# Branch B's product by seven half-size products per column pair, its weight sums in DRAM, and moved stores and bounds

## The chip, the cores and the metric

One core of a Trainium2 chip runs the kernel. The metric is the device time of one execution in microseconds (us). Each core has a matrix engine (TensorE, PE in the profile, with its weight loads as PEld), a vector engine (DVE), a scalar engine (ACT), GpSimd (POOL) and a queue engine (SP) that here only issues DMAs. Every engine works through its own instructions in order and waits on semaphores for the others.

## The reference

One layer of a trunk, on x of 512 × 2048 in float32. Two branches share an RMS-normalised input h: a gated DeltaNet (A) and a convolution module (B). What matters here:

```python
u = jax.nn.glu(glu_in, axis=-1)
u = causal_depthwise_conv(u, w_dw[i]) + b_dw[i]
u = jax.nn.silu(layernorm(u, ln_g[i], ln_b[i])) * jax.nn.silu(z_b)
y_b = u @ w_br_b[i]

gate_a, gate_b = jnp.split(jax.nn.sigmoid(gate_logits + b_gate[i]), N_BRANCHES, axis=-1)
mixed = (gate_a * y_a + gate_b * y_b) @ w_out[i]
x = x + rmsnorm(mixed, g_post[i])

e = p[i] @ w_ple_proj[i]
x = x + rmsnorm(jax.nn.sigmoid(x @ w_ple_gate[i]) * e, g_ple[i])
```

y_a, made by branch A, is `o_a @ w_br_a`. All weights of these products are 2048 × 2048.

## The kernel before

**Arithmetic.** Every product is made of three matmuls on split operands. A float32 operand becomes a high part (a cast on ACT, line 126 for a weight) and a low part (the rest, a subtraction on DVE, line 127); high × high, high × low and low × high are added up in PSUM. A weight piece of 128 × 512 goes SP load (`raw`, three buffers of two pieces) → ACT → DVE into a ring of four pieces `w`; `next_piece()` keeps three made ahead of the one in use.

**Stages.** The load of x, its norm, and p · w_ple_proj (up to 46 us; the product e is kept in SBUF and stored to `pe_dram` by sixteen DMAs on POOL's queue, line 309); the gate and z projections; the heads of branch A with the projections of q, k and v (565 to 1480); GLU and depthwise convolution (to about 1830); branch A's product; layer norm; branch B's product (1902 to 2085); the out product with w_out; the last stage with w_ple_gate.

**Seven products.** The gate and z projections and the out product are already made, per pair of column blocks, of seven half-size products instead of eight: with 512 rows as two halves and the columns as two, sums of operand blocks (S1 to S4) meet sums of weight blocks. For the out product the weight sums are formed beforehand in DRAM: `presum` (lines 1057 and 1062) copies and adds blocks of w_out with 64 DMAs on POOL's queue during the heads (48 read w_out, 16 copy a sum), one per 30 matmuls. The operand blocks come from the merged gate result `mixed` (called gt): `turned` transposes it through PE (tp, line 1275), `combine_low` and `combine_high` (lines 1288 to 1314) form A11, S1 to S4 and the casts (oph, line 1260; opl, line 1262). The product itself is f, lines 1430 to 1432, with weight pieces of 128 × 1024 (wsp, lines 1411 and 1412).

**Branch B before.** `branch()` is the plain product: four column blocks j in the order 0, 2, 1, 3; each of 16 steps takes one weight piece for four row tiles × three matmuls, twelve in all (yp, lines 1136, 1138, 1140). `evac_yb` multiplies by the gate (line 1246) and adds to `mixed` (line 1250). Its operands u come from the layer norm: a sum by a matmul with ones (sum_ps, 1189), mean and variance (1196 to 1204), a diagonal matrix dg (1211), the inverse deviation spread by a matmul (rstd_ps, 1216, at 1872.8), then for each of 16 channel tiles a product with it (1220), silu on ACT (1221), the product with zb (1225), the cast (1227) and the low part (1229).

**Order.** Work beside the matmuls is written as generators: `spawn(gen, period)` enters one, and every matmul calls `tick()`, which steps each generator once per so many matmuls. The Tile context then schedules each engine's instructions; `pin` (keep_in_program_order) holds one where the program has it. `split_mixed()`, the generator of the combine parts, is spawned after the first column block of branch B (period 10) and carried to its end in the out product's opening by `stepper`. There the order is: pair 0's P1 and P7, pair 1's P1, then the rest of pair 0, then Q5, P6, P3, P2, P7, Q4 of pair 1. `post(LOW)`, which norms the first rows and transposes them (line 1521), is stepped under pair 1's P7 and Q4.

Of the kernel before, what the change touches and what calls it, by code (L numbers as in the profile page):

```python
# [81 lines left out]
def _body(ctx, tc, A, out):  # L82
# [155 lines left out]
    def load_x():  # L238
        with tc.tile_pool(name="xin", bufs=1) as xin, tc.tile_pool(name="xps", bufs=6, space=PSUM) as xps:
# [68 lines left out]
            for (j, tt), e in e_sb.items():  # L308
                nc.gpsimd.dma_start(pe_dram[j, tt], e)
# [426 lines left out]
    def head_scan(g, hh, G):  # L736
# [56 lines left out]
        for tt in range(NTT):  # L793
            nc.tensor.transpose(po[:, tt].rearrange("p x i -> p (x i)"), O[:, tt, :], ident)
# [384 lines left out]
    def layer_norm():  # L1179
# [9 lines left out]
        mm(pm, ones, acc[0], start=True, stop=True)  # L1189
# [26 lines left out]
        mm(rstd, ones, dg, start=True, stop=True)  # L1216
# [27 lines left out]
    def evac_yb(j, tt, ps):
        gt = gate_b[tt][j]
        nc.vector.tensor_tensor(gt, ps, gt, ALU.mult)
        if tt == NTT - 1:
            for t in range(NTT):
                m = mixed[t][j]
                nc.vector.tensor_tensor(m, m, gate_b[t][j], ALU.add)  # L1250
            added[j] = NTT


# [74 lines left out]
    def load_gate_b(j):  # L1328
        for tt in range(NTT):
            gate_b[tt][j] = s2.tile([P, T], F32, tag="s2", name="gb")  # L1330
            nc.sync.dma_start(gate_b[tt][j], g_dram[1, tt, j])

    def wanted(k):
        while uT[min(k + 1, NK - 1)] is None:
            next(norm)

    mix = split_mixed()
    for n, j in enumerate((0, 2, 1, 3)):
        for q in range(4):
            if q == 1:  # L1340
                jobs.append(lambda j=j: load_gate_b(j))
            branch(A["w_br_b"], j, q, uT, evac_yb, wanted if n == 0 else None)
        if n == 0:
            jobs.append(lambda: finish())
            jobs.append(lambda: spawn(mix, 10, "mix"))
# [11 lines left out]
    LOW, HIGH, ALL = (0, 1), (2, 3), (0, 1, 2, 3)  # L1357
    SLOT, HP_, S3_ = (slots, "s"), (hpool, "h"), (s3, "s3")

    def unit(home, name, dt=F32):  # L1360
        return home[0].tile([P, T], dt, tag=home[1], name=name)
# [144 lines left out]
    def post(tts, xr):  # L1506
# [7 lines left out]
        for j in range(4):  # L1514
            if j < 3:
                with_x(j + 1)
            for k2 in (2 * j, 2 * j + 1):
                ps = bank()
                for n in range(4):
                    k = 2 * k2 + n // 2  # L1520
                    nc.tensor.transpose(ps[:, n * P:(n + 1) * P], x1[tts[n % 2]][j][:, (k % 4) * P:(k % 4 + 1) * P], ident)
# [232 lines left out]
```

## Time and profile before

| what | value |
|---|---|
| median of 3 runs | 2430.66 us (2429.46 to 2431.43) |
| the profiled execution | 2433.04 us, span 2431.3 |
| granted TensorE clock, mean | 0.998 |
| busy: PE, PEld, DVE, ACT, POOL | 99%, 82%, 75%, 48%, 19% |

The profile is that of one execution. Busy times are sums over instructions; matmuls overlap one another (one lasts 0.39 us, the next begins 0.23 us after it), so PE's pace is read from counts in a window of time, not from durations. A line such as `L1250 ... x3` in a timeline is three instructions in a row, with the time from the first's start to the last's end. In square brackets stands the idle time ahead of an instruction, and what ended it.

### The profile page before, as it was taken

How to read it: one execution, taken by the hardware profiler on the slowest of the kernel's cores; microseconds unless marked ns; L12 is line 12 of the kernel's file. 1: busy time of each engine (PE TensorE's matmuls, PEld its weight loads, DVE VectorE, ACT ScalarE, POOL GpSimd, SP SyncE). 2: the span in 40 equal slices, each digit the busy share in tenths (PEclk: the TensorE clock that was granted, in tenths of full speed). 3: DMA queues.
4: the chain of work that ended last, by engine and by line, in shares of the span. 5: the costliest groups of instructions: out<-in, count | busy, mean ns of one | idle time of the engine just before them, and what ended most of it. 6: DMA issues, size and time to landing. Idle time of an engine off the chain costs nothing.

```text
span 2431.3 us, 33577 instructions
## 1 busy us (share of the span) xinstructions
PE 2411.2 (99%) x11966; PEld 1985.0 (82%) x11966; DVE 1811.8 (75%) x3376; ACT 1163.3 (48%) x2331; POOL 449.8 (19%) x449
## 2 busy tenths in 40 slices
PE   9999999999999999999999999999999999999998
PEld 7888888887888888888888887888887888888886
DVE  7877888776778686777868678999998654667644
ACT  6555455555554545454554544454424433554532
POOL 2001100011112121121101001998840000000000
PEclk9999999999999999999999999999999999999999
DMA  6477766764364463554323221443434332664552
GB/s 264 158 193 212 200 199 202 208 171 161 130 174 143 139 192 127 151 161 136 116 76 102 76 84 69 156 139 104 163 128 164 128 129 100 230 226 164 193 175 77
DMA packets 133145, 371.80 MB, mean 153 GB/s; under 512 B 14833, under 2 KB 23281, under 8 KB 132465
## 3 DMA queue, kind: packets, MB, share of 16 engines
q1 hardware_dynamic: 116848, 315.12, 38.2%
q0 software_dynamic: 13824, 50.34, 9.4%
q10 hardware_dynamic: 2304, 4.20, 0.5%
q8 instruction: 94, 1.54, 0.2%
q14 instruction: 75, 0.61, 0.1%
HBM read 338.14 MB, written 65.01 MB: 166 GB/s over the span
## 4 chain that ended last, share of the span: by engine, by line
PE 92%; DVE 4%; DMA 2%; issue 1%; ACT 1%; POOL 0%; SPq 0%; DVEq 0%; POOLq 0%; ACTq 0%
PE g L185 14%; PE g L187 14%; PE g L183 14%; PE zp L475 6%; PE zp L473 6%; PE zp L474 6%; PE yp L1140 4%; PE yp L1138 4%; PE yp L1136 4%; PE f L1431 2%; PE f L1432 2%; PE f L1430 2%; PE f L1605 2%; PE f L1603 2%; PE f L1604 2%; PE psB L760 1%
## 5 line engine op out<-in xcount | busy, mean ns | idle before, releaser
L185 PE MATMUL g<-hl,w 128*128 128x512 f32 x1536 | 610.5, 397 | 0.0
L187 PE MATMUL g<-hh,w 128*128 128x512 f32 x1536 | 609.0, 397 | 0.0
L183 PE MATMUL g<-hh,w 128*128 128x512 f32 x1536 | 608.3, 396 | 0.0
L126 ACT CAST w<-raw 128x512 fp32r<-128x512 f32 x580 | 356.2, 617 | 525.6 <-PE g L187 258.5
L127 DVE TENSOR_TENSOR w<-raw,w 128x512 fp32r<-128x512 f32 x466 | 321.4, 694 | 194.7 <-ACT w L126 192.2
L185 PEld LDWEIGHTS g<-hl,w 128*128 128x128 f32 x1536 | 289.2, 188 | 55.4 <-issue 1.2
L183 PEld LDWEIGHTS g<-hh,w 128*128 128x128 f32 x1536 | 289.3, 188 | 53.9
L187 PEld LDWEIGHTS g<-hh,w 128*128 128x128 f32 x1536 | 289.3, 188 | 53.9 <-POOL w L127 0.3
L1006 DVE SCALAR_TENSOR_TENSOR uc<-up,vec,uc 128x497 f32<-128x497 f32 (+29 forms) x390 | 282.3, 734 | 13.2 <-ACT uc L985 1.9
L127 POOL TENSOR_TENSOR w<-raw,w 128x512 fp32r<-128x512 f32 x114 | 146.8, 1305 | 59.6 <-ACT w L126 57.8
L707 DVE SCALAR_TENSOR_TENSOR cv<-g,vec,cv 128x511 f32<-128x511 f32 x144 | 106.6, 740 | 41.4 <-ACT cv L705 41.1
L1138 PE MATMUL yp<-w,uh 128*128 128x512 f32 x256 | 100.4, 392 | 0.0
L1136 PE MATMUL yp<-w,uh 128*128 128x512 f32 x256 | 100.3, 393 | 0.1
L1140 PE MATMUL yp<-w,ul 128*128 128x512 f32 x256 | 100.4, 392 | 0.0
L1138 PE MATMUL yp<-w,oh 128*128 128x512 f32 x256 | 100.1, 391 | 0.0
L1140 PE MATMUL yp<-w,ol 128*128 128x512 f32 x256 | 99.5, 391 | 0.0
L1136 PE MATMUL yp<-w,oh 128*128 128x512 f32 x256 | 99.1, 389 | 0.0
L893 DVE TENSOR_TENSOR prod<-UT,VT 128x2 f32<-128x2 f32 (+30 forms) x248 | 87.3, 352 | 6.5
L718 POOL COPY kq<-kc 128x512 f32<-128x512 f32 x16 | 11.5, 721 | 383.9 <-ACT kc L716 225.5
L1028 POOL TENSOR_TENSOR uc<-uc,pr 128x511 f32<-128x511 f32 (+29 forms) x60 | 76.1, 1269 | 8.3 <-ACT pr L1027 7.7
L1430 PE MATMUL f<-wsp,oph 128*128 128x512 f32 x192 | 75.5, 393 | 0.0
L1603 PE MATMUL f<-w,xh 128*128 128x512 f32 x192 | 75.5, 393 | 0.0
(399 smaller groups left out, 4883.6 us busy)
## 6 DMA issues: line engine op xcount, KB each, us to landing
raw<-in_w_in SPq DMA_DIRECT2D x194, 512.0 KB, 3.3
wo_sums<-in_w_out POOLq DMA_DIRECT2D x48, 512.0 KB, 7.7
raw<-in_w_ple_gate SPq DMA_DIRECT2D x40, 512.0 KB, 3.3
raw<-in_w_br_a SPq DMA_DIRECT2D x32, 512.0 KB, 3.3
raw<-in_w_br_b SPq DMA_DIRECT2D x32, 512.0 KB, 3.3
raw<-in_w_ga SPq DMA_DIRECT2D x24, 512.0 KB, 5.1
raw<-in_w_gb SPq DMA_DIRECT2D x24, 512.0 KB, 5.1
raw<-in_w_z SPq DMA_DIRECT2D x22, 512.0 KB, 4.6
```

The costliest lines, as they stand in the source:

```text
L126: nc.scalar.copy(hi, rq)
L127: low_part[0].tensor_tensor(lo, rq, hi.bitcast(F32), ALU.subtract)
L183: mm(ps, wh, rh, start=(k == 0), stop=False)
L185: mm(ps, wh, rl, start=False, stop=False)
L187: mm(ps, wl, rh, start=False, stop=(k == NK - 1))
L473: mm(ps[pr][t], lh, wh, start=q + n == 0, stop=False)
L474: mm(ps[pr][t], ll, wh, start=False, stop=False)
L475: mm(ps[pr][t], lh, wl, start=False, stop=q == 3 and n == 1)
L1006: pin(nc.vector.scalar_tensor_tensor(y[:, s:], u[:, 0:T - s], vv(w0 + TAPS - 1 - s), y[:, s:], ALU.mult, ALU.add))
L1136: mm(ps[tt], lh[:, b], wh, start=k == 0, stop=False)
L1138: mm(ps[tt], lh[:, b], wl, start=False, stop=False)
L1140: mm(ps[tt], ll[:, b], wh, start=False, stop=k == NK - 1)
```

## The change

It makes these edits:

1. The sixteen stores of e leave `load_x` for a generator `stores()` in the next phase, each pinned.
2. Pins on the first matmuls of sw_ps, sum_ps, rstd_ps, on one transpose of po and on the transposes of `post`; one `yield` becomes `yield 14`.
3. Branch B's product is made of seven half-size products for each of the two column pairs. P1, P2 and Q4 run both pairs interleaved; Q5, P6, P7 and P3 follow for pair 0, then for pair 1. A weight piece serves two row tiles, six matmuls. The layer norm gives, for the first eight channel tiles, split halves (ua), and behind its loop the operands S1 to S4 (half-size sums `usf` on DVE, each pair of halves then cast and split, oph and opl). Results of a product are kept (`bsnap`, copied by ACT), combined, gated and added to `mixed` on DVE.
4. w_br_b is laid out in blocks, and its sums are formed in DRAM by the same `presum`, ahead of those of w_out: 64 more DMAs on POOL's queue, one per 24 matmuls.
5. `split_mixed` does all four `combine_low` and then all four `combine_high`; it is spawned after pair 0's P3 (period 7).
6. In the out product pair 1's P7 moves up, behind its P1, and its result is kept (s7b); `stepper` takes two steps in the first P1.

The core of the diff:

```diff
-            for (j, tt), e in e_sb.items():
-                nc.gpsimd.dma_start(pe_dram[j, tt], e)
...
+        def stores():
+            for (j, tt), e in e_sb.items():
+                pin(nc.gpsimd.dma_start(pe_dram[j, tt], e))
+                yield
+        spawn(stores(), 12, "form")
         spawn(gen, 7, "form")
...
-        mm(pm, ones, acc[0], start=True, stop=True)
+        pin(mm(pm, ones, acc[0], start=True, stop=True))
...
+    sums_b = dram.tile([2, 4, 4, P, 1024], F32, name="wb_sums")
+
+    def presums():
+        yield from presum(A["w_br_b"], sums_b)
+        yield from presum(WO, sums)
...
-            jobs.append(lambda: spawn(presum(WO, sums), 30, "presum"))
+            jobs.append(lambda: spawn(presums(), 24, "presum"))
...
-            uh = low(0, "uh")
-            nc.scalar.copy(uh, u)
-            ul = low(LOP if i < 33 - LOP else 0, "ul")
-            nc.vector.tensor_tensor(ul, u, uh.bitcast(F32), ALU.subtract)
+            if i < 8:
+                if i % 2 == 0:
+                    ua[i // 2] = low(0, "uh"), low(0, "ul")
+                c = slice((i % 2) * 256, (i % 2) * 256 + 256)
+                uh, ul = [x[:, c] for x in ua[i // 2]]
+                nc.scalar.copy(uh, u[:, LO])
+                nc.vector.tensor_tensor(ul, u[:, LO], uh.bitcast(F32), ALU.subtract)
+            else:
+                uh, ul = low(0, "uh"), low(LOP if i == NK - 1 else 0, "ul")
+                nc.scalar.copy(uh, u)
+                nc.vector.tensor_tensor(ul, u, uh.bitcast(F32), ALU.subtract)
             uT[i] = (uh, ul)
             yield 6
+        us1, us3 = [None] * 4, [None] * 4
+        for name in ("S1", "S2", "S3", "S4"):
+            for k2 in range(4):
...
+                for kk, c in halves(k2):
+                    u, v = u_t[kk], u_t[kk + 8]
+                    a, b, op = {"S1": (u[:, HI], v[:, HI], ALU.subtract), "S2": (t[:, c], u[:, LO], ALU.subtract),
+                                "S3": (u[:, LO], u[:, HI], ALU.subtract), "S4": (t[:, c], v[:, LO], ALU.add)}[name]
+                    nc.vector.tensor_tensor(t[:, c], a, b, op)
+                yield 4
+                uS[name][k2] = sw_split(*((s2, "s2") if name == "S1" else (hpool, "h") if name == "S3" else (lop, "lop")), t)
+                yield 6
...
+    def fin_b(tts, j, cs):
+        for tt, c in zip(tts, cs):
+            nc.vector.tensor_tensor(c, c, gate_b[tt][j], ALU.mult)
+        for tt, c in zip(tts, cs):
+            m = mixed[tt][j]
+            nc.vector.tensor_tensor(m, m, c, ALU.add)
+            added[j] += 1
...
     def split_mixed():
-        for part, k2 in ((combine_low, 0), (combine_low, 1), (combine_high, 0), (combine_high, 1),
-                         (combine_low, 2), (combine_low, 3), (combine_high, 2), (combine_high, 3)):
-            yield from part(k2)
+        for part in (combine_low, combine_high):
+            for k2 in range(4):
+                yield from part(k2)
...
+            for q in range(4):
+                for x, (jp, pr) in enumerate(products):
+                    for n in range(2):
+                        kk = 2 * q + n
+                        wh, wl = next_piece()
+                        for t in range(2):
+                            lh, ll = b_opnd(OPND[pr], kk, t)
+                            mm(ps[x][t], lh, wh, start=kk == 0, stop=False)
+                            tick()
+                            mm(ps[x][t], ll, wh, start=False, stop=False)
+                            tick()
+                            mm(ps[x][t], lh, wl, start=False, stop=kk == 7)
+                            tick()
...
+        def p7(jp):
+            def f(ps):
+                u = b_u[jp]
+                u3 = [tt_b(u["u2"][t], ps[t], u["u2"][t], ALU.add) for t in range(2)]
+                fin_b(HIGH, 2 * jp + 1, [tt_b(u["s5"][t], u["s5"][t], u3[t], ALU.subtract) for t in range(2)])
+                fin_b(HIGH, 2 * jp, [tt_b(u["s4"][t], u["s4"][t], u3[t], ALU.add) for t in range(2)])
+            return f
...
+        b_job([(0, "P1"), (1, "P1")], p1, [(S2_, LOW, 0), (S2_, LOW, 2)])
+        b_job([(0, "P2"), (1, "P2")], p2)
+        b_job([(0, "Q4"), (1, "Q4")], q4)
+        jobs.append(lambda: finish("norm"))
+        for jp in range(2):
+            b_job([(jp, "Q5")], q5(jp))
+            b_job([(jp, "P6")], p6(jp), [(LO_, HIGH, 2 * jp + 1), (LO_, HIGH, 2 * jp)])
+            b_job([(jp, "P7")], p7(jp))
+            b_job([(jp, "P3")], p3(jp), [(LO_, LOW, 2 * jp + 1)])
+            if jp == 0:
+                jobs.append(lambda: spawn(mix, 7, "mix"))
...
-    for jp, prs in ((0, ("P1", "P7")), (1, ("P1",)), (0, ("P2", "Q5", "P6", "P3", "Q4")), (1, ("Q5", "P6", "P3", "P2", "P7", "Q4"))):
+    for jp, prs in ((0, ("P1", "P7")), (1, ("P1", "P7")), (0, ("P2", "Q5", "P6", "P3", "Q4")), (1, ("Q5", "P6", "P3", "P2", "Q4"))):
...
-    ps = run(("P1",), stepper(gen))
+    ps = run(("P1",), stepper(gen, 2))
...
     pgen = post(LOW, xr)
-    ps = run(("P7",), stepper(pgen))
-    u3 = [add(u2[t], ps["P7"][t], u2[t]) for t in range(2)]
+    u3 = [add(u2[t], s7b[t], u2[t]) for t in range(2)]
...
-        "w_br_b": _tm_tiles(a["w_br_b"]),
+        "w_br_b": _sw_tiles(a["w_br_b"]),
```

The scheduler's order at three places. First POOL at the start of the kernel, before (xrs are the powers of the norm of x, each after its tile's statistics; the DMA rows are the stores of e):

```order
L309 DMA pe_dram<-e_sb 128x512 x2
L265 ISA
L265 TENSOR_TENSOR xrs<-xms,mhalf_c 128x1 x2
L309 DMA pe_dram<-e_sb 128x512 x4
L265 TENSOR_TENSOR xrs<-xms,mhalf_c 128x1
L309 DMA pe_dram<-e_sb 128x512 x6
```

And POOL there with the change:

```order
L101 MEMSET mhalf_c 128x8
L265 ISA
L265 TENSOR_TENSOR xrs<-xms,mhalf_c 128x1 x4
L507 DMA pe_dram<-e_sb 128x512 x16
L419 DMA zt<-in_w_z 128x512 x16
L419 DMA zt<-in_w_ga 128x512 x16
```

The stores, which stood between the powers, now stand behind all four of them and ahead of the z weights' sums.

Second DVE at the end of the layer norm, before (ur and ul are the tiles of u and their low parts, w weight pieces, zb the silu of z_b):

```order
L1220 TENSOR_TENSOR ur_16804<-ur_16804,rstd_ps_17098 128x512
L127 TENSOR_TENSOR w_17584<-raw_17582,w_17584 128x512
L127 TENSOR_TENSOR w_17587<-raw_17582,w_17587 128x512
L1225 TENSOR_TENSOR ur_16804<-ur_16804,zb_17438 128x512
L127 TENSOR_TENSOR w_17624<-raw_17622,w_17624 128x512
L1229 TENSOR_TENSOR ul_17508<-ur_16804,uh_17506 128x512
L127 TENSOR_TENSOR w_17627<-raw_17622,w_17627 128x512
```

And DVE there with the change (usf are the sums S1 to S4, opl their low parts):

```order
L1231 TENSOR_TENSOR ur_16869<-ur_16869,rstd_ps_17163 128x512
L127 TENSOR_TENSOR w_17631<-raw_17629,w_17631 128x512
L127 TENSOR_TENSOR w_17634<-raw_17629,w_17634 128x512
L1236 TENSOR_TENSOR ur_16869<-ur_16869,zb_17495 128x512
L1262 TENSOR_TENSOR usf_17639<-ur_16498,ur_16524 128x256
L1262 TENSOR_TENSOR usf_17639<-ur_16501,ur_16676 128x256
L1262 TENSOR_TENSOR usf_17656<-ur_16505,ur_16855 128x256
L1247 TENSOR_TENSOR ul_17564<-ur_16869,uh_17563 128x512
L1262 TENSOR_TENSOR usf_17656<-ur_16508,ur_16869 128x256
L127 TENSOR_TENSOR w_17661<-raw_17659,w_17661 128x512
L1305 TENSOR_TENSOR opl_17590<-usf_17581,oph_17588 128x512
```

Behind the last channel tile DVE had only weight pieces to make; now the sums and low parts of the four operands stand between these pieces.

Third DVE at the end of branch B's product, before (gb the gates, gt the merged result, yp the banks of PSUM, wsp the out product's weight pieces):

```order
L1246 TENSOR_TENSOR gb_18612<-yp_18496,gb_18612 128x512
L1246 TENSOR_TENSOR gb_18614<-yp_18497,gb_18614 128x512
L1250 TENSOR_TENSOR gt_17260<-gt_17260,gb_18610 128x512
L1250 TENSOR_TENSOR gt_17262<-gt_17262,gb_18612 128x512
L1250 TENSOR_TENSOR gt_17264<-gt_17264,gb_18614 128x512
L1412 TENSOR_TENSOR wsp_18840<-raw_18825,wsp_18839 128x1024
L1412 TENSOR_TENSOR wsp_18846<-raw_18827,wsp_18845 128x1024
L1262 TENSOR_TENSOR opl_18867<-sf_17846,oph_18865 128x512
L1262 TENSOR_TENSOR opl_18976<-tp_18963,oph_18974 128x512
```

And DVE at the end of pair 1's P7 with the change (bsnap the kept and combined results):

```order
L1294 TENSOR_TENSOR gt_17321<-gt_17321,bsnap_18750 128x512
L1294 TENSOR_TENSOR gt_17323<-gt_17323,bsnap_18752 128x512
L1433 TENSOR_TENSOR bsnap_18235<-bsnap_18235,bsnap_17859 128x512
L1433 TENSOR_TENSOR bsnap_18237<-bsnap_18237,bsnap_17861 128x512
L1291 TENSOR_TENSOR bsnap_18235<-bsnap_18235,gb_18758 128x512
L1291 TENSOR_TENSOR bsnap_18237<-bsnap_18237,gb_18760 128x512
L1294 TENSOR_TENSOR gt_16927<-gt_16927,bsnap_18235 128x512
L1294 TENSOR_TENSOR gt_16929<-gt_16929,bsnap_18237 128x512
L127 TENSOR_TENSOR w_18990<-raw_18985,w_18990 128x512
L127 TENSOR_TENSOR w_19026<-raw_19024,w_19026 128x512
L1305 TENSOR_TENSOR opl_19013<-tp_18998,oph_19011 128x512
L1305 TENSOR_TENSOR opl_19017<-tp_19003,oph_19015 128x512
```

The gates and adds of two column blocks (bsnap with gb, then gt) stand here ahead of the last weight pieces (w) of branch B and of the first low parts that combine_high makes from the transposes (opl from tp). Before, the last gates stood beside the out product's first pieces.

More of the change, by code (lines that the diff above doesn't have):

```diff
@@ L663, in beta_decay @@
         nc.vector.tensor_scalar(neg_eg.rearrange("p t h -> p (t h)"), eg, -1.0, None, ALU.mult)
-        yield
+        yield 14
         pw = wps.tile([P, T], F32, tag="w", name="sw_ps")
-        mm(pw[:, 0:n], cc(C_SWAP), eg, start=True, stop=True)
+        pin(mm(pw[:, 0:n], cc(C_SWAP), eg, start=True, stop=True))
         nc.vector.tensor_copy(eg_sw.rearrange("p t h -> p (t h)"), pw[:, 0:n])
@@ L793, in head_scan @@
         for tt in range(NTT):
-            nc.tensor.transpose(po[:, tt].rearrange("p x i -> p (x i)"), O[:, tt, :], ident)
+            turn = nc.tensor.transpose(po[:, tt].rearrange("p x i -> p (x i)"), O[:, tt, :], ident)
+            if tt == 0 and g == NH // 2 - 1:
+                pin(turn)
         yield
@@ L1215, in layer_norm @@
         rstd = ups.tile([P, T], F32, tag="u", name="rstd_ps")
-        mm(rstd, ones, dg, start=True, stop=True)
+        pin(mm(rstd, ones, dg, start=True, stop=True))
         yield 6
@@ L1225, in layer_norm @@
             nc.vector.tensor_tensor(u, u, zb[i], ALU.mult)
[L1226 to L1229 removed]
+            if i < 8:
[9 more added lines that the diff above has]
+                nc.vector.tensor_tensor(ul, u, uh.bitcast(F32), ALU.subtract)
             uT[i] = (uh, ul)
             yield 6
+        us1, us3 = [None] * 4, [None] * 4
+        for name in ("S1", "S2", "S3", "S4"):
+            for k2 in range(4):
+                if name == "S1":
+                    us1[k2] = hp("usf")
+                elif name == "S3":
+                    us3[k2] = hp("usf")
+                t = us3[k2] if name == "S3" else us1[k2]
+                for kk, c in halves(k2):
[6 more added lines that the diff above has]
+                yield 6
     def load_zb(i):
@@ L1235, in load_zb @@
         nc.sync.dma_start(zb[i], zb_dram[i])
+    ua = [None] * 4
+    uS = {n: [None] * 4 for n in ("S1", "S2", "S3", "S4")}
     norm = layer_norm()
@@ L1242, in _body, with unit, gate_in @@
     added = [0] * 4
[L1244 to L1251, printed above, removed]
+    SLOT, HP_, S2_, LO_ = (slots, "s"), (hpool, "h"), (s2, "s2"), (lop, "lop")
+    def unit(home, name, dt=F32):
+        return home[0].tile([P, T], dt, tag=home[1], name=name)
+    def gate_in(home, tts, j):
+        for tt in tts:
+            gate_b[tt][j] = unit(home, "gb")
+            nc.sync.dma_start(gate_b[tt][j], g_dram[1, tt, j])
+    def fin_b(tts, j, cs):
[5 more added lines that the diff above has]
+            added[j] += 1
     AW = {n: [None] * 4 for n in ("A11", "S1", "S2", "S3", "S4")}
@@ L1326, in split_s3 @@
             yield
[L1328 to L1331, printed above, removed]
+    WB = A["w_br_b"]
+    WHICH_B = {"P1": (WB, B11), "P2": (WB, B21), "P3": (WB, B22),
+               "Q5": (sums_b, T1), "P6": (sums_b, T2), "P7": (sums_b, T3), "Q4": (sums_b, T4)}
     def wanted(k):
-        while uT[min(k + 1, NK - 1)] is None:
+        while uT[k] is None:
             next(norm)
-    mix = split_mixed()
@@ L1338, in _body, with b_opnd @@
-    for n, j in enumerate((0, 2, 1, 3)):
-        for q in range(4):
[L1340 to L1345, printed above, removed]
+    def b_opnd(name, kk, t):
+        if name in ("A12", "A22"):
+            wanted(kk + 8)
+            c = (256 if name == "A22" else 0) + t * P
+            return [x[:, c:c + P] for x in uT[kk + 8]]
+        c = (kk % 2) * 256 + t * P
+        if name == "A11":
+            wanted(kk)
+            return [x[:, c:c + P] for x in ua[kk // 2]]
+        while uS[name][kk // 2] is None:
+            next(norm)
+        return [x[:, c:c + P] for x in uS[name][kk // 2]]
@@ new lines, in _body, with b_bank, b_job, job @@
+    b_banks = [0]
+    def b_bank():
+        b_banks[0] += 1
+        return yps.tile([P, T], F32, tag="y", name="yp")
+    def b_job(products, done_, gates=()):
+        for q in range(4):
+            for jp, pr in products:
+                W, blk = WHICH_B[pr]
+                prep_src.append(W[jp, blk, q])
+        def job():
+            for g_ in gates:
+                gate_in(*g_)
+            ps = [[b_bank() for _ in range(2)] for _ in products]
+            for q in range(4):
[11 more added lines that the diff above has]
+                            tick()
+            done_(*ps)
+        jobs.append(job)
@@ L1346, in _body @@
+    mix = branch_b()
     lnp_ctx = ExitStack()
@@ L1356, in _body @@
     fsm = ctx.enter_context(tc.tile_pool(name="fsm", bufs=1))
[L1357 to L1361, printed above, removed]
+    ALL = (0, 1, 2, 3)
+    S3_ = (s3, "s3")
     def bcast_row(src, j, home=S3_):
@@ L1547, in _body @@
     ps = run(("P1",), stepper(gen, 2))
+    s1b = [snap(SLOT, x) for x in ps["P1"]]
+    ps = run(("P7",), stepper(gen, 2))
     drain(gen)
-    s1b = [snap(HP_, x) for x in ps["P1"]]
+    s7b = [snap(S3_, x) for x in ps["P7"]]
     ps = run(("P2",))
```

40 lines of the change are left out of this document (39 added, 1 removed).

## The prediction

> **What bounds the kernel now.** I read the page's head first, then the chain that ended last, then TensorE's rate stretch by stretch. The page gives the span, the busy shares, and the chain by engine:
>
> ```profile
> span 2431.3 us, 33577 instructions
> PE 2411.2 (99%) x11966; PEld 1985.0 (82%) x11966; DVE 1811.8 (75%) x3376; ACT 1163.3 (48%) x2331; POOL 449.8 (19%) x449
> PE 92%; DVE 4%; DMA 2%; issue 1%; ACT 1%; POOL 0%; SPq 0%; DVEq 0%; POOLq 0%; ACTq 0%
> ```
>
> TensorE (PE) is the bound almost throughout, so a matmul taken away is worth its pitch if nothing else then comes late. The windows give that pitch, and show how near the vector engine (DVE) is to being the bound around branch B's product (columns: window, length, then busy time and count of PE, PEld, DVE, ACT, POOL; granted clock; DMA share; GB/s):
>
> ```profile
> 300.00:400.00 100.00, 100.00 (x443) 82.81 (x442) 82.22 (x132) 52.61 (x88) 7.06 (x8) 1.00 0.65 195
> 1880.00:1900.00 20.00, 20.00 (x90) 16.57 (x89) 18.55 (x32) 14.20 (x23) 0.00 (x0) 1.00 0.57 196
> 1900.00:1920.00 20.00, 19.88 (x86) 15.46 (x85) 16.91 (x28) 10.79 (x17) 0.00 (x0) 1.00 0.47 161
> 1920.00:1940.00 20.00, 20.00 (x90) 16.57 (x89) 4.85 (x7) 4.96 (x8) 0.00 (x0) 1.00 0.28 93
> 2080.00:2100.00 20.00, 20.00 (x94) 16.54 (x93) 16.30 (x22) 11.16 (x16) 0.00 (x0) 1.00 0.68 261
> 2100.00:2120.00 20.00, 19.75 (x92) 16.20 (x91) 18.38 (x28) 14.97 (x22) 0.00 (x0) 1.00 0.77 279
> ```
>
> 443 matmuls in 100 us are 225.7 ns each. Branch B's product begins near 1902. Just ahead of it DVE is full (18.55 of 20: the layer norm's tail), in its middle nearly idle (4.85), and at its end, where the operands of the out product are formed, full again (18.38). So DVE's spare time lies in the middle, and the change adds DVE work at both ends. All waits of PE in before over 0.25 us that bear on the change:
>
> ```profile
> PE xp L313 <- DVE hl L317: 3.6, 1, 3.6
> PE rstd_ps L1216 <- DVE dg L1211: 0.7, 1, 0.7
> PE f L1521 <- DVE c L1511: 0.6, 1, 0.6
> PE tp L1275 <- DVE sf L1314: 0.3, 1, 0.3
> ```
>
> Only the first is worth naming; the seams around branch B are crossed today almost without a stall.
>
> **The matmuls: −21.7 us.** Branch B was 4 column blocks × 16 × 4 × 3 = 768 matmuls and becomes 7 products × 2 column pairs × 8 × 2 × 3 = 672. 96 × 225.7 ns = 21.7 us. The f products and the 64 turning transposes keep their counts.
>
> **The stores at the start: −4.8 us.** The stretch where PE waits 3.6 us (windows, the chain, the DMA issues, and four transposes of the chain at full clock):
>
> ```profile
> 20.00:30.00 10.00, 10.00 (x51) 8.38 (x50) 8.99 (x19) 8.39 (x14) 6.28 (x10) 1.00 1.03 414
> 38.00:40.00 2.00, 2.00 (x9) 1.47 (x8) 2.00 (x4) 2.00 (x5) 0.00 (x0) 0.70 0.63 188
> 40.00:42.00 2.00, 2.00 (x9) 1.70 (x8) 2.00 (x4) 0.42 (x1) 0.00 (x0) 0.50 0.27 111
> 20.59 14.56 DMA raw<-in_w_in
> 43.31 0.44 PE xp L313 x4
> pe_dram<-e_sb POOLq DMA_DIRECT2D x16, 256.0 KB, 7.8
> 27.24 0.57 POOL L265 TENSOR_TENSOR xrs<-xms,mhalf_c 128x1 f32<-128x1 f32 x1 [0.59 <-DVE xms L263]
> L421 POOL DMA_DIRECT2D zt<-in_w_z x16: 865/890/1180, 115.8 to 216.8; - x16
> ```
>
> The DMA engines are full (1.03, 414 GB/s), and a weight load takes 14.56 us. The sixteen stores are 4.2 MB, 10 us of that bandwidth, ahead of or beside the last loads. With the change they stand behind the fourth power on POOL, which runs at 27.24 now and a little sooner then, so the loads land before PE asks. What goes is the 3.6 us and the half clock that follows it: 2 × 0.30 + 2 × 0.50 = 1.6 us. That is 5.2 at best; POOL issues eight of the stores without a wait, 2 MB or 5 us of bandwidth that may still meet the last load, so the low end is 1. I take 4.8, near the upper end, since the loads then have 10 us in hand against those 5. The stores' reader comes only in the last stage, and POOL's next work behind them, the z weights' sums, runs from 115.8 us on (the last row).
>
> The Trainium skill ("TensorE: Matmul & The Clock Gate", Part 1) puts the half clock down to an idle window of about 3.4 us; the trace agrees, with 0.50 after the one wait of 3.6. By it the clock is lost at any new wait of that length; that is a rival below.
>
> **The pins** (the waits for sw_ps, po, sum_ps, rstd_ps and the post transposes): in the order of the program these matmuls stand where they stood, so 0, and ±0.3 by the waits listed.
>
> **The norm's tail and the first two products: +7.8 us.** This needs DVE's pace when it runs without a break (first rows: consecutive starts; then the tail):
>
> ```profile
> 2100.04 2.36 DVE L1412 TENSOR_TENSOR wsp<-raw,wsp 128x1024 fp32r<-128x1024 f32 x2
> 2102.32 0.68 DVE L1262 TENSOR_TENSOR opl<-sf,oph 128x512 fp32r<-128x512 f32 x1
> 2102.92 1.22 DVE L1412 TENSOR_TENSOR wsp<-rw,wsp 128x1024 fp32r<-128x1024 f32 x1
> ...
> 2111.04 0.74 DVE L1306 TENSOR_TENSOR sf<-cm,tp 128x256 f32<-128x256 f32 x2
> 2111.70 1.22 DVE L1412 TENSOR_TENSOR wsp<-raw,wsp 128x1024 fp32r<-128x1024 f32 x1
> ...
> 1872.70 0.69 DVE L127 TENSOR_TENSOR w<-raw,w 128x512 fp32r<-128x512 f32 x1
> 1874.00 1.88 DVE L1220 TENSOR_TENSOR ur<-ur,rstd_ps 128x512 f32<-128x512 f32 x3 [0.62 <-PE rstd_ps L1216]
> 1882.73 1.40 DVE L1225 TENSOR_TENSOR ur<-ur,zb 128x512 f32<-128x512 f32 x2 [1.44 <-ACT ur L1221]
> 1902.11 0.68 DVE L1147 TENSOR_TENSOR gt<-yp,gt 128x512 f32<-128x512 f32 x1
> 1902.71 1.28 DVE L1225 TENSOR_TENSOR ur<-ur,zb 128x512 f32<-128x512 f32 x2
> 1903.91 0.68 DVE L1147 TENSOR_TENSOR gt<-yp,gt 128x512 f32<-128x512 f32 x1
> 1915.61 0.69 DVE L127 TENSOR_TENSOR w<-raw,w 128x512 fp32r<-128x512 f32 x1
> ```
>
> One 128x512 takes 0.68 alone and starts 0.60 before the next (2102.32 to 2102.92); two 128x1024 start 2.28 before what follows, 1.14 each; two 128x256 take 0.66, 0.33 each. In before DVE works from 1872.70 to 1916 and then rests. In the order of the change, from that same weight piece (at 1872.70) to the piece that P2's fifth step needs stand 125 DVE instructions: 85 of 128x512 (29 weight pieces, 32 norm products, 8 full low parts, 12 low parts of the sums, 4 gates of branch A) and 40 of 128x256 (8 half low parts, 32 of the sums S1 to S4). 85 × 0.60 + 40 × 0.33 = 64.2, with the two waits quoted (0.62, 1.44) 66.3: done at 1939.0. PE stands 250 matmuls behind the rstd matmul (about 1873.9) there: 1930.3 at full pace. It waits 8.7, of which before has about 0.9 (x86 against x90 in 1900 to 1920): +7.8. Bounds 5 and 12: two breaks like the 1.44 fewer or three more.
>
> **End of pair 0's P7: +2.9 us.** Behind P7's last matmul stand 16 DVE instructions of 128x512 (differences, gates, adds, the piece between): 16 × 0.60 + 0.7 of handing over = 10.3 before the transposes of the merged columns and the next piece are served; PE comes there after some 33 matmuls, 7.4. The pieces made ahead (3 × 6 × 0.2257 = 4.1) lie inside those 7.4. Bounds 0 and 5.
>
> **End of pair 1's P7, into the out product: +10.0 us.** With combine_high for all four column pairs now behind branch B, DVE has 38 × 0.60 + 12 × 0.33 + 6 × 1.14 = 33.6 us from P7's end to the last S4 sum that the 97th matmul after it waits for; PE's 97 matmuls and 16 transposes (0.11 each, from the four in 0.44) take 21.9 + 1.8 = 23.7. Before crossed this at 0.3. Bounds 6, if a tenth of the block is done while P7 still runs, and 14, at full single durations.
>
> **The rest.** The last stage's post(LOW) loses P7 as cover: +0.5 over the 0.6 quoted. The 64 sums of w_br_b go over POOL's queue in the heads stage: there PE is as dense with such copies as without (0.52 and 0.25 of the DMA engines):
>
> ```profile
> 900.00:1100.00 200.00, 200.00 (x1205) 165.73 (x1204) 147.38 (x363) 100.73 (x266) 32.47 (x40) 1.00 0.52 156
> 1200.00:1400.00 200.00, 200.00 (x1203) 165.79 (x1203) 147.72 (x351) 103.16 (x268) 15.77 (x19) 1.00 0.25 85
> L126 ACT CAST w<-raw 128x512 fp32r<-128x512 f32 x122 | 75.3, 620 | 135.3 <-PE yp L1140 106.7 <-PE f L1605 12.6 <-DVE w L127 8.2
> raw<-in_w_br_b SPq DMA_DIRECT2D x28, 512.0 KB, 3.2
> ```
>
> So 0. The raw loads double in rate (a piece now serves 6 matmuls, 1.35 us, and a load two pieces, 2.7 us) with three buffers: 8.1 us a round against 3.2 to land and two casts and two subtractions, 2.5. Covered; if it weren't, this is a ring that runs late in the whole product. For handshakes I don't see, +0.5. ACT's snapshots replace DVE reads of PSUM and lie under its idle time (it waits 106.7 us for PE there).
>
> **Sum.** −21.7 − 4.8 + 7.8 + 2.9 + 10.0 + 0.5 + 0.5 = −4.8. The profiled run took 2433.04, giving 2428.2; it lies 2.4 over the median of the three runs, 2430.66, so on the median's footing 2425.9, said as 2426. A change of under 0.2% (4.9 us) can't be told from none: faster means under 2425.8, slower over 2435.5. The forecast falls on that edge, and that is why its chances split.
>
> **The rivals.**
>
> *DVE can't hold the 0.60 pitch (chance 0.11).* The pitch holds between instructions that wait for nothing; the new ones wait for ACT's cast of the same tile each time. If each costs its single duration (0.68, 0.41, 1.22), the seams grow by 125 instructions' worth, 85 × 0.08 + 40 × 0.08 = 10.0, then 16 × 0.08 = 1.3, then 4.5: 15.8 in all, 2442, slower than before. It decides once two thirds of that comes. Against it: from 1902.11 to 1903.91 three instructions of two lines, on tiles that PE and ACT had written, took 1.80; for it: the 1.44 quoted. The Trainium skill ("VectorE: DVE Perf Modes", on SBUF-source latency) gives (N+151)/0.96 ns for such an add, 691 at 512; the trace agrees for a single one (0.68 to 0.69 us), not for a row of them.
>
> *The seams cost half (0.14).* If PE finds more made ahead than I counted, 20.7 of seams are 10 and the time is 2415; none at all would be 2404. For it: before crossed similar blocks of eight instructions with no wait. Against it: DVE's queue is in order and the counts are fixed.
>
> *The stores still collide (0.11).* Eight go out unhindered; if they meet the last weight load, the start keeps its 3.6 and its clock: 2431. It is also the case in which that edit doesn't do what it says.
>
> *The clock drops at the new waits (0.12).* The first and third seams may hold a wait of over 3.5 us; each then costs 2 us as at 38 to 42 (x9 for x18): 2430. Against it: PE would be slow where DVE is the bound anyway.
>
> **Chances and range.** The forecast has 0.52, spread over 2420 to 2432, half of it on each side of the edge. Faster: 0.26 + 0.14 + 0.02 + 0.03 (parts of the last two) = 0.45; same: 0.26 + 0.09 + 0.09 = 0.44; slower: 0.11. The range takes in the forecast, the two 2430 cases, half of the second rival, and the edge of the first: 2415 to 2437.
>
> **What would show it.** In the profile of the change: no wait at xp, granted clock 1.00 in 36 to 44, the stores issued after 24 us; 96 fewer PE instructions and the same 225.7 ns in 300 to 400; DVE over 90% busy from the norm to the first third of P2 and a sum of PE waits there near 8 us, released by DVE w; near 10 us between the last P3 and the second f product, released by gates, wsp and the S sums; under 3 elsewhere in the product. It is wrong if PE waits on raw, ring or ACT through the middle of the product, if the seams sum to under 12 or over 30 us, or if the time falls to under 2415.

## The result, and the profile after

The change took 2441.3 us (median of 6 runs, 2440.89 to 2442.5) against 2430.5 before (6 runs, 2429.46 to 2431.96): 10.8 us slower, ratio 1.0047, 95% interval 1.0036 to 1.0058. Forecast were 2426.0 and a range of 2415 to 2437. The matmuls went as said and the start got quicker; PE then waited at more places, and longer, than the sum had.

The head of the page of the change:

```profile
span 2439.4 us, 33786 instructions
PE 2399.4 (98%) x11870; PEld 1972.0 (81%) x11870; DVE 1877.9 (77%) x3500; ACT 1206.9 (49%) x2409; POOL 496.5 (20%) x513
```

96 PE instructions are gone (11966 to 11870), yet the span is longer. PE's waits (line and what released it; us in all, times, the longest):

```profile
PE tp L1318 <- DVE gt L1294: 6.0, 3, 3.2
PE yp L1415 <- ACT bsnap L1429: 4.1, 1, 4.1
PE f L1574 <- DVE wsp L1554: 4.0, 1, 4.0
PE yp L1419 <- DVE w L127: 3.6, 4, 1.5
PE yp L1415 <- DVE gt L1158: 2.5, 1, 2.5
...
PE pk L825 <- DVE ke L830: 1.4, 1, 1.4
...
PE xp L311 <- DVE hl L315: 0.6, 1, 0.6
...
PE pq L842 <- DVE E_mk L692: 0.5, 1, 0.5
```

The wait at the start went from 3.6 to 0.6. In and behind branch B's product five new kinds add up to 20.2 us. The windows show where (same columns as before; the last but two is the granted clock):

```profile
1900.00:1920.00 20.00, 14.66 (x52) 10.26 (x52) 19.32 (x37) 12.15 (x21) 0.00 (x0) 0.91 0.41 126
1920.00:1940.00 20.00, 15.95 (x63) 12.57 (x63) 18.44 (x40) 12.12 (x22) 0.00 (x0) 0.91 0.47 162
...
2020.00:2040.00 20.00, 16.78 (x72) 13.31 (x72) 16.66 (x30) 7.85 (x15) 0.00 (x0) 0.91 0.45 147
...
2060.00:2080.00 20.00, 17.12 (x71) 13.32 (x70) 17.04 (x29) 8.18 (x13) 0.00 (x0) 0.91 0.45 136
2080.00:2100.00 20.00, 16.04 (x68) 12.95 (x67) 19.25 (x31) 11.11 (x17) 0.00 (x0) 0.91 0.62 230
```

From 1900 to 1940 PE ran 115 matmuls where before ran 176 (x86 and x90): 61 × 0.2257 = 13.8 us lost. DVE is full there, as forecast, and it keeps the pitch that the prediction counted on, also where low parts stand between weight pieces (0.60 us from start to start):

```profile
1912.22 0.68 DVE L127 TENSOR_TENSOR w<-raw,w 128x512 fp32r<-128x512 f32 x1
1912.83 0.68 DVE L1305 TENSOR_TENSOR opl<-usf,oph 128x512 fp32r<-128x512 f32 x1
1913.43 0.68 DVE L127 TENSOR_TENSOR w<-raw,w 128x512 fp32r<-128x512 f32 x1
```

The clock is 0.91 in five windows: a mean of 0.91 over 20 us is some 3.5 us at half clock, 1.7 us of PE's work, and the windows of 2 us place each such stretch right behind a wait. The chain that made the longest wait of the first seam, in rows of the timeline of DVE, ACT and PE:

```profile
1932.16 0.75 DVE L1262 TENSOR_TENSOR usf<-ur 128x256 f32<-128x256 f32 x2
```
```profile
1932.95 0.62 ACT L1303 CAST oph<-usf 128x512 fp32r<-128x512 f32 x1 [1.43 <-DVE usf L1262]
1933.48 2.04 ACT L1429 COPY bsnap<-yp 128x512 f32<-128x512 f32 x4
```
```profile
1934.11 0.50 PE L1415 MATMUL yp<-w,uh 128*128 128x512 f32 x1 [4.05 <-ACT bsnap L1429]
```

P1's last matmul began at 1929.7. Its banks had to be copied by ACT before P2 could write them; ACT's queue is in order, and ahead of the copies stood a cast of an operand sum that DVE had not finished. The sum is the last of S3, which P7 reads first: pair 0's P7 begins 288 matmuls later. So an operand that was not yet needed held up the bank that PE needed at once.

### The profile page after: what moved, and what is told of

It reads as the page before. It is cut to its first block, busy times and chain, and to the rows that moved or that the text cites. A ratio compares the mean times of both kernels' runs of the same rounds, so it can differ in the third digit from the quotient of the medians.

```text
span 2439.4 us, 33786 instructions
## 1 busy us (share of the span) xinstructions
PE 2399.4 (98%) x11870; PEld 1972.0 (81%) x11870; DVE 1877.9 (77%) x3500; ACT 1206.9 (49%) x2409; POOL 496.5 (20%) x513
## 5 line engine op out<-in xcount | busy, mean ns | idle before, releaser
L126 ACT CAST w<-raw 128x512 fp32r<-128x512 f32 x628 | 385.9, 618 | 495.9 <-PE g L187 261.5
L127 DVE TENSOR_TENSOR w<-raw,w 128x512 fp32r<-128x512 f32 x514 | 355.1, 698 | 148.6 <-ACT w L126 146.3
L1748 PE MATMUL f<-w,xh 128*128 128x512 f32 x192 | 75.1, 393 | 1.0 <-DVE xl L1669 1.0
L1749 PE MATMUL f<-w,xh 128*128 128x512 f32 x192 | 75.1, 391 | 0.3 <-DVE w L127 0.3
L1573 PE MATMUL f<-wsp,opl 128*128 128x512 f32 x192 | 75.3, 392 | 0.0
L1750 PE MATMUL f<-w,xl 128*128 128x512 f32 x192 | 74.9, 390 | 0.0
```

The lines of the kernel that those rows point to most:

```text
L126: nc.scalar.copy(hi, rq)
L127: low_part[0].tensor_tensor(lo, rq, hi.bitcast(F32), ALU.subtract)
L1573: mm(ps, ll, wh[:, c], start=False, stop=False)
L1748: mm(ps[tt], lh, wh, start=k == 0, stop=False)
L1749: mm(ps[tt], lh, wl, start=False, stop=False)
L1750: mm(ps[tt], ll, wh, start=False, stop=k == NK - 1)
```

## A second profile of before

The kernel before, unchanged, profiled again (run 2430.57, near its median; the first profile's run took 2433.04):

> The kernel before, unchanged, for a second profile. The profiled run of before took 2.4 us over the median. If the wait at the start (3.6 us at xp and the half clock after it) is as long here, 5.2 us is what the store edit is worth and e1_stores lost 2.4 elsewhere. If it is shorter by about 2 us in a run near the median, the excess of that profile lay in the stall itself, and the edit is worth about 2.8.

Its wait at the start, and the two windows that in the first profile had the half clock:

```profile
PE xp L313 <- DVE hl L317: 3.1, 1, 3.1
```
```profile
38.00:40.00 2.00, 2.00 (x15) 1.72 (x15) 2.00 (x5) 1.95 (x4) 0.00 (x0) 1.00 0.85 293
40.00:42.00 2.00, 2.00 (x17) 1.79 (x16) 2.00 (x4) 1.42 (x3) 0.00 (x0) 1.00 0.10 41
```

x15 and x17 at clock 1.00, where the first profile had x9 and x9 at 0.70 and 0.50. The half clock there was that one execution's: 1.6 us of it, and the wait that is 0.5 longer, make 2.1 of its 2.4 us over the median. Measured against this second profile the 10.6 us of span (2439.4 less 2428.8) fall as follows, by the starts of the same matmuls:

| stretch | before, second profile | the change | difference |
|---|---|---|---|
| to sw_ps | 579.6 | 577.0 | -2.6 |
| sw_ps to the first po | 157.5 | 159.3 | +1.8 |
| po to rstd_ps | 1133.1 | 1133.3 | +0.2 |
| rstd_ps to the last f | 370.5 | 378.5 | +8.0 |
| last f to the end | 188.1 | 191.3 | +3.2 |

## The experiments

**The stores alone.** Before, with the stores moved as in the change:

```diff
-            for (j, tt), e in e_sb.items():
-                nc.gpsimd.dma_start(pe_dram[j, tt], e)
...
+        spawn(stores(), 12, "form")
```

> The kernel before with the store edit alone. If the gain at the start is what the profile of the change shows (its first matmul of sw_ps 5.2 us earlier) and stays, the time is 5.2 us under before, about 2425.3. Rival: a later stage gives it back (in the change 1.8 us are lost again before 740 us, and this edit may be what moves the heads); then 2428 to 2430.

2427.92 against 2430.73, 2.8 us less (ratio 0.9991, 0.9982 to 1.0001). The interval just holds no change, but the rows agree: sw_ps begins at 576.7, 2.9 before the second profile of before, and 157.6 us later po. In all fourteen profiles with this edit sw_ps begins at 576.4 to 578.0, in the two without it at 579.6 and 582.2. So the edit is worth 2.8, within about one, and nothing is given back. My alternative put the remainder of the 5.2 down to a later loss; it had never been there.

**The sums put off.** The change, with 150 matmuls between the norm's loop and the sums S1 to S4:

```diff
         us1, us3 = [None] * 4, [None] * 4
+        yield 150
```

> The change, with the forming of the sums S1 to S4 put off by 150 matmuls, so that DVE has them to do after the norm's tail and not inside it. Theory (DVE is late at the norm's tail, and ACT's copies of P1's banks stand in its queue behind casts that wait for these sums): of the 14.7 us lost between 1900 and 1940 some 12 go, about 2429, and the half-clock stretches there go too. Rival (the same DVE work only moves, and the next products wait for it): the loss comes back later in the product, about 2438 to 2441.

2430.34, 11.0 under the change and level with before (0.9998, 0.9989 to 1.0007). In 1900 to 1940:

```profile
1900.00:1920.00 20.00, 18.30 (x77) 13.73 (x76) 15.69 (x26) 11.44 (x20) 0.00 (x0) 1.00 0.50 184
1920.00:1940.00 20.00, 20.00 (x90) 16.57 (x89) 18.47 (x38) 14.99 (x27) 0.00 (x0) 1.00 0.65 211
```

167 matmuls instead of 115, the clock full, and the waits for bsnap and branch A's gt gone. DVE works off the same sums beside the next products (18.47 in the second row); from 1940 to 2000 PE waits once, 0.9 us for a weight piece, as it does in the change (0.8). The theory held: it was when the sums were formed, not that they were.

**P7's two column blocks exchanged.** The change, gating block 2jp ahead of 2jp + 1:

```diff
-                fin_b(HIGH, 2 * jp + 1, [... s5 - u3 ...])
                 fin_b(HIGH, 2 * jp, [... s4 + u3 ...])
+                fin_b(HIGH, 2 * jp + 1, [... s5 - u3 ...])
```

> The change, with the two column blocks behind P7 gated and added in the other order, so that the block whose transposes come next is done six DVE instructions (3.6 us) earlier. Theory (each wait of 2.5 us or more costs itself and 1.7 us of half clock after it): the two waits for gt of 3.2 and 2.7 us go with their half-clock stretches, together 9 us: about 2432. Rival (the next thing DVE owes, w or wsp, is late by nearly as much): 2438 to 2440.

2441.41: no gain, and a little over the rival's 2438 to 2440. The waits:

```profile
PE yp L1419 <- DVE w L127: 7.1, 5, 3.1
...
PE tp L1318 <- DVE gt L1294: 2.7, 1, 2.7
```

What left gt (6.0 to 2.7) came to w (3.6 to 7.1). The rival's mechanism held: DVE's differences, gates and adds, fourteen instructions, still stand in one piece ahead of the next weight piece (2065.9 to 2074.3 at pair 1).

**The out product's order as before.** The change with pair 1's P7 back ahead of Q4:

```diff
-(1, ("P1", "P7")), (0, ...), (1, ("Q5", "P6", "P3", "P2", "Q4"))
+(1, ("P1",)), (0, ...), (1, ("Q5", "P6", "P3", "P2", "P7", "Q4"))
```

> The change, with the out product's order as before (pair 1's P7 last but one, covering post of the low rows). Theory (the last stage lost 3.3 us for want of that cover, of which 0.5 would be the waits): about 2438.3, 3 us under the change, and the stretch from the last f product to the end as before. Rival (P7 early also covers the seam into the out product, which then loses more): 2441 or more.

2437.87, 3.4 under the change, as the theory had it. The rows below give, for one line of the out product (f<-wsp) and one of the gate product behind it (f<-w), the start of its first and of its last matmul; first the change, then the old order:

```profile
L1574 PE MATMUL f<-wsp,oph x192: 388/389/480, 2102.2 to 2248.1; 128*128 128x512 f32 x192
L1748 PE MATMUL f<-w,xh x192: 387/389/496, 2250.2 to 2385.7; 128*128 128x512 f32 x192
```
```profile
L1574 PE MATMUL f<-wsp,oph x192: 387/389/398, 2100.9 to 2247.2; 128*128 128x512 f32 x192
L1747 PE MATMUL f<-w,xh x192: 388/389/481, 2247.5 to 2381.5; 128*128 128x512 f32 x192
```

From the out product's last matmul (2248.1) to the gate product's first (2250.2) the change does only transposes and waits for them; with the old order that gap is 0.3 (2247.2 to 2247.5). The gate product's matmuls then spread over 135.5 us against 134.0.

**Fillers in the waits.** The change, with nine matmuls ahead of the first transposes of combine_low and of combine_high:

```diff
+            if kk == 0:
+                fill(9)
             ps = turned(kk)
```

> The change, with nine matmuls that compute nothing of the output (2.0 us) put ahead of the transposes where PE waits 3.2 and 2.7 us for gt. Theory (each wait of 2.5 us or more is followed by a stretch of 3.4 us at half clock, which costs 1.7 us by itself): the fillers lie inside the waits, the two half-clock stretches go, and the time falls by 3.4 to about 2438. Rival (behind such a wait DVE is late anyway, so a slow PE costs nothing): no gain, 2441 to 2442.

2443.23, 1.9 over the change. The first group ran at 2031.9, 8 us behind its wait, which ended at 2024.0, and cost its 2.0 (the expectation of the next run has it ahead of the wait; the rows show it behind). The second stood where it should, and that wait for gt shrank from 2.7 to 0.4. Windows of 2 us there, of the change and then with the fillers:

```profile
2074.00:2076.00 2.00, 1.58 (x5) 0.90 (x6) 2.00 (x5) 0.74 (x2) 0.00 (x0) 0.75 0.00 0
2076.00:2078.00 2.00, 2.00 (x6) 1.57 (x5) 2.00 (x4) 0.95 (x2) 0.00 (x0) 0.50 0.73 248
```
```profile
2074.00:2076.00 2.00, 1.63 (x8) 1.01 (x7) 2.00 (x5) 0.62 (x1) 0.00 (x0) 1.00 0.00 0
2076.00:2078.00 2.00, 1.67 (x8) 1.05 (x9) 2.00 (x4) 1.08 (x3) 0.00 (x0) 1.00 0.00 0
```

PE kept its clock, and the next wait, for wsp, grew from 4.0 to 4.4. Ahead of the stretch the run with fillers was 1.7 us behind the change (the transposes after the wait at 2075.95 against 2074.24), behind that next wait 0.85 (2092.29 against 2091.44): in this pair of profiles the half-clock stretch gave back 0.9 of its 1.7. With both groups pinned directly ahead of the transposes:

```diff
+            if tt == 0 and kk in (0, 8):
+                pin(turn)
```

> As e6_fill, with the transposes pinned so that both groups of nine matmuls stand directly ahead of the waits for gt (in e6_fill the first group ran 20 matmuls ahead of its wait and cost its 2.0 us; the second lay inside the wait and no half clock followed). Theory: both stretches of half clock go, and nothing is paid for the fillers: 2441.3 less 3.4, 2438. Rival (what follows waits for DVE whatever PE's clock): 2441 to 2442.

2445.05. The first group now ran at 2033.4, behind a wait of 4.1 for w that took the place of that for gt. Of the 3.8 us over the change, 1.9 lie elsewhere in the profile: sw_ps to po took 161.2 against 159.3, with a half-clock stretch from 636.1 in the heads. Neither run got faster, against the theory of each. So the fillers showed that a busy PE keeps its clock; what a half-clock stretch costs in the end they leave open, beyond the 0.9 above.

**Low parts on POOL.** As e2_late_sums, with every second low part of a weight piece on POOL, and the same with two edits undone:

```diff
-            low_part[0].tensor_tensor(lo, rq, hi.bitcast(F32), ALU.subtract)
+            low_part[q % len(low_part)].tensor_tensor(lo, rq, hi.bitcast(F32), ALU.subtract)
```

> The change with the sums put off (as in e2_late_sums, 2430.3), and the low part of every second weight piece of branch B's product made on POOL and not on DVE. Theory (DVE's queue is what is late at the seams): the waits for w and gt that are left (8.3 us) shrink by a third to a half and one or two half-clock stretches go: about 2425. Rival (a low part takes POOL 1.3 us against 0.6, so pieces come late): 2431 or more.

> As e7_pool, with the out product's order as before (worth 3.4 alone) and the edit at sw_ps (yield 14 and its pin) undone. Theory: the gains add, and if that edit is what cost 1.8 us in the heads, about 5 us under e7_pool: 2420. Rival: the heads' loss is from the copies of w_br_b and stays, then 2422; or the order of the out product gives less with a quicker seam, then 2424.

2449.80 and 2443.18: 19.5 and 12.8 over e2_late_sums. The rival held, and more than it said. PE's longest wait, 6.4 us, was for one low part on POOL, which took 8.01 us beside a row of DVE instructions that ran without a break until 1941.2; most others on POOL took 1.29:

```profile
1934.28 8.01 POOL L127 TENSOR_TENSOR w<-raw,w 128x512 fp32r<-128x512 f32 x1 [3.18 <-ACT w L126]
```

DVE became slower beside POOL too (below). Between the two runs the edits are worth 6.6, not 5. In e8_best sw_ps begins at 577.0 and po at 734.5: 157.5 us again, against 159.3 in the change, and the wait at pk is gone. The same stretch is 157.5 to 157.6 in all nine profiles without that edit, with the copies of w_br_b or without, and 158.9 to 161.2 in the seven with it. So the `yield 14` and the pin at sw_ps, undone together, are what the heads lost 1.8 by; which of the two, no run shows.

**Three edits together.** The sums put off, the out product's order as before, the edit at sw_ps undone:

> The change with three edits undone or moved: the sums put off (alone 2430.3), the out product's order as before (3.4 alone), the edit at sw_ps undone (1.5 in the rows of e8_best up to 740 us). If they add: 2425.4. Left are the waits at the two ends of P7 (some 10 us for gt and wsp) and their half-clock stretches. Rival (a quicker start of the product or another order only lengthens a later wait): 2428 or more.

2426.11 against 2430.37 (0.9984, 0.9975 to 0.9993): they add within a microsecond.

**Half of P7's block on POOL.** As e9_three, block 2jp on DVE, block 2jp + 1 on POOL:

```diff
+                for t in range(2):
+                    nc.gpsimd.tensor_tensor(u["s5"][t], u["s5"][t], u3[t], ALU.subtract)
+                fin_b(HIGH, 2 * jp + 1, u["s5"], nc.gpsimd)
```

> As e9_three, and behind P7 the column block whose transposes come next is gated and added first on DVE, and the other one's difference, gate and add (six instructions a pair) go to POOL, which is idle there. Theory (DVE's block of 16 instructions is what PE waits for behind P7, for gt, w and wsp): 3.6 us of DVE go from each of the two seams, the waits for gt go, that for wsp shrinks, and two half-clock stretches go: 9 to 12 us under e9_three, 2414 to 2417. Rival (POOL slows DVE beside it, as in e7_pool, or its 1.3 us an instruction bring gt late): 2425 or more.

2430.78, 4.7 over e9_three. The rival held; DVE's rows beside POOL's work, and POOL's:

```profile
2002.89 1.79 DVE L1434 TENSOR_TENSOR bsnap<-bsnap 128x512 f32<-128x512 f32 x1
...
2006.47 1.77 DVE L1292 TENSOR_TENSOR bsnap<-bsnap,gb 128x512 f32<-128x512 f32 x1
```
```profile
2002.36 1.77 POOL L1471 TENSOR_TENSOR bsnap<-bsnap 128x512 f32<-128x512 f32 x1 [134.58 <-ACT w L126]
```

**P7's block broken up, on DVE.** As e9_three, block 2jp first; block 2jp + 1 by a generator, a step in nine matmuls:

```diff
+                def rest():
+                    for t in range(2):
+                        tt_b(u["s5"][t], u["s5"][t], u3[t], ALU.subtract)
+                        yield
+                        fin_b(HIGH[t:t + 1], 2 * jp + 1, u["s5"][t:t + 1])
+                        yield
+                spawn(rest(), 9, "fin")
```

> As e9_three, and behind P7 DVE does first the column block whose transposes come next; the other block's six instructions (difference, gate, add for two row tiles) are handed to a generator that steps once in nine matmuls, so that weight pieces stand between them. All stays on DVE. Theory (PE waits behind P7 for DVE's unbroken block): the waits of 3.2 and 2.9 us for gt go, and their half-clock stretches; the wait of 4.0 for wsp stays, since DVE has the same work before it: 2426.1 less 6 to 8, about 2419. Rival (DVE's work up to the out product's second piece is the limit, as in e3_swap): 2424 to 2426.

2423.68 against 2430.08: 0.9974, 0.9964 to 0.9983. It beats both kernels, by 6.4 and 17.6 us, though by less than the theory's 6 to 8 against e9_three (2.4). Its waits:

```profile
PE f L1583 <- DVE wsp L1563: 7.6, 1, 7.6
...
PE tp L1319 <- DVE gt L1295: 0.6, 1, 0.6
```

Those for gt fell from 6.3 in e9_three to 0.6. At pair 0 that is a gain, with no wait over 0.3 left there; at pair 1 it came back at wsp, 4.0 to 7.6, with 1.5 more for a sum (sf). That points to two mechanisms: at pair 0 the unbroken block, at pair 1 the whole of DVE's work.

**combine_high held back.** As e12_defer, combine_high only in the out product; and that with pair 1's P7 moved up as in the change:

```diff
+        yield 300
         for k2 in range(4):
             yield from combine_high(k2)
```

> As e12_defer, and combine_high is held back until the out product's first products, whose stepper carries it. Theory (the wait for wsp is DVE's combine_high ahead of the first wsp pieces): the 4.0 go with their half clock, but the three products that then cover combine_high have 33 us of PE for 36 us of DVE, so some 3 come back: 2 to 4 under e12_defer. Rival: the later products wait for A12 and A22 instead, no gain or a loss.

> As e13_hold, with the out product's order of the change (pair 1's P7 moved up), which gives 10.8 us more of PE to cover combine_high and loses 3.4 in the last stage. Theory: against e13_hold the cover is worth up to 3 and the last stage costs 3.4, so the same time within 2. Rival: the seam is already covered in e13_hold, then 3.4 slower.

2427.75 and 2429.92, 4.1 and 6.2 over e12_defer. In e13_hold wsp costs 1.7, but a later wait takes its place:

```profile
PE f L1583 <- DVE sf L1358: 5.9, 1, 5.9
PE tp L1319 <- DVE sf L1358: 4.6, 1, 4.6
...
PE f L1585 <- DVE wsp L1565: 1.7, 1, 1.7
```

The rival held in kind: PE then waits at the sums (sf) of the last blocks. Moving P7 up cost 2.2 here and didn't cover that.

## Why the prediction was wrong, point by point

Two steps failed above all. The norm's tail, +7.8, was worked out along one path only, from DVE's weight pieces to PE; in the run PE was held there first by PSUM banks that ACT and DVE had not freed, and lost 13.8. And the half clock behind the new waits was left out of the sum, because only waits of over 3.5 us were thought to cause it; waits of 2.5 to 4.1 us were each followed by one, five in all. The terms one by one:

- **96 matmuls, -21.7.** Right: 96 fewer, and x443 in 300 to 400 us as before.
- **The start, -4.8.** Right in kind, too large: 2.8. The step that failed is the footing. I took one execution's wait and half clock for what every run has, and then took off the whole 2.4 us between that execution and the median as if it lay outside the term. Most of it lay inside. The stores met no load: twelve, not eight, went out in a row from 27.5 us on, and the wait at xp was 0.6.
- **The pins, 0.** Wrong: 1.8 in the heads, by the edit at sw_ps. "Stand where they stood" was true of sw_ps, po, sum_ps and rstd_ps; the matmul behind sw_ps (r_ps) stood nine matmuls later and I gave that no price. DVE then came late for pq and pk (0.5 and 1.4). My list of waits over 0.25 us was short there too: it lacks po (1.5), sw_ps (0.6) and sum_ps (0.4), which the pins touch.
- **The norm's tail, +7.8.** Measured 13.8. The DVE sum held: 1939.0 forecast for the piece, 1935.8 once the earlier start (rstd_ps at 1869.6, not 1872.8) is taken off, and that piece was made at 1937.3 to 1938.0. What failed is that I followed only weight pieces from DVE to PE. PE was stopped earlier, by PSUM banks: 2.5 us for branch A's last gates behind norm work on DVE, 4.1 for ACT's copies behind casts that wait for DVE. Weight pieces made it wait only 2.8 there, not 8.7. Two stretches of half clock, 3.4 us of PE's work, came on top.
- **Pair 0's P7, +2.9.** A wait of 3.2, and 1.7 of half clock: 4.9. The wait was sized rightly.
- **Pair 1's P7, +10.0.** Waits of 2.7 and 4.0, 0.4 of small ones, and two half-clock stretches of 1.7: 10.5. The total fits, the make-up doesn't: I had it all as waits.
- **Last stage, +0.5.** 3.2; e4_out_back gives back 3.4. I counted one wait and not the transposes that then stood bare between the products.
- **The copies in DRAM, 0, and loads of pieces, 0.** Borne out as far as the rows go: po to rstd_ps differs by 0.2, and no wait of PE in the product was ended by a load.

All waits in and around the product come to 20.4 us; the seams were sized at 20.7. That the totals agree is partly luck: the tail has more waits than forecast (9.3 us) and pair 1's end fewer (7.1), and in the tail they are for other things. The rest of the miss is what the sum left out: five stretches of 3.4 us at half clock, 1.7 us of PE's work each or 8.5 together by the count of matmuls (what removing one alone gains is open, as above), the last stage, the heads and the smaller gain at the start. None of the prediction's own signs of being wrong came true, since they watched the waits and not the clock behind them. The clock was among the rivals, with a chance of 0.12, two stretches and the remark that DVE would be the bound anyway. The rival that forecast slower, DVE without its 0.60 pitch, gave 2442, close to the 2441.3 measured, but by chance: in the change DVE's rows keep that pitch. A slip besides: with no seams at all the sum gives 2405, not 2404.

## What to carry to other kernels

Work that has no hurry should be kept out of every in-order queue that PE's next bank or piece goes through: the same sums cost 11 us in the norm's tail and next to nothing 150 matmuls later. When a sum of waits is made, follow each PSUM bank to whoever frees it, through that engine's queue, and price the clock behind each wait of 2 us or more. Take the difference between a profiled execution and the median as a question about the very stall that the change removes, and take a second profile of before if there is any.

## What the runs showed of the hardware

A DVE instruction that reads two tensors from SBUF took 1.75 to 1.79 us beside POOL's work, against 0.68 alone (rows under e10_poolfin). One that reads PSUM was not slowed: in e7_pool two of them took 1.27 together while POOL made a low part.

```profile
1960.82 1.27 DVE L1435 TENSOR_TENSOR bc<-yp,bsnap 128x512 f32<-128x512 f32 x2
```
```profile
1960.48 1.54 POOL L127 TENSOR_TENSOR w<-raw,w 128x512 fp32r<-128x512 f32 x1 [1.34 <-ACT w L126]
```

The Trainium skill ("SBUF — State Buffer", "SBUF: two separate sides") describes a pair of ports for which an instruction with two SBUF inputs and a GpSimd one lock each other out; the trace agrees, in both directions (POOL's 8.01 us under e7_pool).

The half clock followed waits shorter than I had thought. Waits of 2.5, 2.7, 3.2, 4.0 and 4.1 us each had a stretch behind them in the change; one of 3.1 at the start of before's second profile had none. Where a wait falls decides. In the trace's record of the clock the five stretches of the change that followed these waits begin at 1904.32, 1935.04, 2023.79, 2074.99 and 2092.06 us: 9, 26, 15 and 5 times 3.413 us apart, and each lasts 3.41. The Trainium skill ("TensorE: Matmul & The Clock Gate", Part 1) has a window of 3.4 us that runs freely; the trace agrees. Here are two such windows around a wait of 2.7 us for gt in the change, then two around the same wait in e4_out_back, where it was 2.4 us and fell across a border:

```profile
2071.58:2074.99 3.41, 0.58 (x3) 0.35 (x4) 3.41 (x7) 0.00 (x0) 0.00 (x0) 1.00 0.00 0
2074.99:2078.40 3.41, 3.40 (x9) 2.43 (x9) 3.41 (x8) 1.69 (x3) 0.00 (x0) 0.50 0.45 154
```
```profile
2069.46:2072.87 3.41, 2.04 (x9) 1.33 (x8) 3.41 (x7) 1.04 (x2) 0.00 (x0) 1.00 0.00 0
2072.88:2076.29 3.41, 2.05 (x9) 1.39 (x10) 3.41 (x7) 1.41 (x3) 0.00 (x0) 1.00 0.08 18
```

PE was idle for 2.8 us of one window in the change, and for 1.4 of each of two in e4_out_back, and only the change lost its clock there. The 3.1 us of before's second profile fell into two windows as 1.9 and 1.2. Over all sixteen profiles, up to 2400 us, every window at full clock in which PE idled 2.04 us or more was followed by one at half clock, and none in which it idled 1.73 or less; between these both occurred.
